# Two parts of the second layer's conditioning, computed in the first layer's routing and at the layer boundary

## Chip, cores and metric

The kernel runs on one core of one Trainium2 chip. The metric is the device time of one execution in microseconds (us). Times are compared by the median of repeated runs; a profile is one further execution, recorded by the hardware profiler.

## What is computed

Two layers of a hybrid backbone over 256 latent tokens and 256 context tokens of 1024 features, all in f32. Cut to what matters here:

```python
for i in range(DEPTH):                                   # DEPTH = 2
    mod = (silu(c) @ ada_w[i] + ada_b[i])[:, None, :]    # conditioning: 1024 x 6144 per layer
    mod_c = silu(c_ctx) @ ada_w[i] + ada_b[i]
    sh1, s1, g1, sh2, s2, g2 = split(mod, 6)             # and the same of mod_c
    px = modulate(rms(x, norm1[i]), sh1, s1) @ w_in[i]   # modulate(h, b, a) = h * (1 + a) + b
    pc = modulate(rms(ctx, norm1[i]), sh1c, s1c) @ w_in[i]
    yx, yc = mixers(px, pc, ...)                         # retention, windowed GQA, global GQA
    x = x + g1 * (yx @ w_out[i])
    hx = modulate(rms(x, norm2[i]), sh2, s2)
    ...                                                  # layer 0: the same for the context
    x = x + g2 * moe(hx, w_router, b_router, w_gate_up[i], w_down[i])   # top 2 of 16 experts
```

The conditioning of a layer is needed in three stages: `sh1, s1` before the input projection, `g1, sh2` after the output projection, `s2, g2` for the router and the end of the experts.

## The kernel before

**Stages.** Each layer runs norm1, the input projection `px` in five column blocks (3, 0, 4, 1, 2), the three mixers, `out_proj` with the router's product at its end, `route`, and the experts (`moe`). Layer 1 needs no context output after the mixers. Large products are made of two rounded halves of each f32 operand and three matmuls (`mm3`, L200 to L202); the halves of a weight page are `hi` on ACT (L190) and `lo` on DVE (L192), for the first `w_in` pages of layer 1 on POOL.

**Weights.** All weights come as pages of 1 MB in one order, the list `stream` that `run` writes; SP issues the loads (L164) in that order, each as soon as a page of SBUF is free. `take` waits for a page, `drop` gives it back and lets `pump` issue the next load. SP is one queue: an instruction of SP that waits holds up all behind it, also the stores `hx` (L1015) of the normalized tokens, which the experts' gather (L1224, POOL) reads back. The list stops at the second expert's pages until the order of the experts is known.

**Conditioning.** `ada_w` of a layer is cut in three thirds of 8 pages: third (l, 0) holds `sh1, s1`, (l, 1) `g1, sh2`, (l, 2) `s2, g2`. A third is 16 small bias matmuls (L362), then 8 steps of four 32-column matmuls (L347; the trace has two records for each) into the tile `adap`, then `ada_done`: a copy `adam` out of PSUM (L401, DVE), four transposes `modT` (L394), and small work on DVE. For third 0 this is `A` and `B` (L407, L409); for third 2 it is a memset and two DMAs of `n2` on POOL, one operation (L418), four DMAs `modd` on POOL and the router matrix `wm` (L429). The table `FILL` says how many steps run in each part of the mixers: thirds (0,1) and (0,2) in layer 0's `px` and attention, (1,0) in its retention (two steps per head), (1,1) in its global attention, and (1,2) in layer 1's `px`.

**Names in the order of work.** `rs` and `ro` (L796, L815) are the score and output products of a retention head, `am` (L800) the masked scores that `ro` reads, `s` the attention scores. `lg` and `lgT` (L956, L1005) are the router's logits and their transposes, `pos` (L1094) the positions of tokens in their experts, `over` (L1133) a number that all engines load before a branch, `fl` (L1294) the first expert's transposes. `fin` (L1566) and `ftmp` (L1577, L1578) end layer 0's experts; `junk` (L475) are the squares of norm1, `xT` (L493) its transposes; `hm` and `hT` (L512 to L519) the modulated input of layer 1, in four pairs of feature blocks; `tab` (L575 to L589) tables of the attention, on POOL.

Of the kernel before, what the change touches and what calls it, by code (L numbers as in the profile page):

```python
# [24 lines left out]
NPAGES = 20  # L25
RING = 6

FILL = [dict(px=1, att=8, ret=2, glb=8), dict(px=1, att=0, ret=0, glb=0)]

# [29 lines left out]
class Kernel:  # L61
    def __init__(self, nc, tc, es, I, out):
        self.nc, self.tc, self.I, self.out = nc, tc, I, out
        pool = lambda name, bufs=1, **k: es.enter_context(tc.tile_pool(name=name, bufs=bufs, **k))
        self.cp = pool("const")
        self.pgs = Pages(pool("pages"), NPAGES)
        self.hip = pool("hi")
        self.sm = pool("small", 2)
        self.ps = pool("psum", space=bass.MemoryType.PSUM)
        self.dr = pool("dram", space=bass.MemoryType.DRAM)  # L70
        self.flight = {}
        self.order = {}
        self.at = None
        self.spare = self.extra = 0
        self.hold = None
        self.owed = []
        self.ev = 0


# [66 lines left out]

    def pump(self):
        g = self.pgs
        while self.stream and (g.ring or self.extra < self.spare and g.open):
            c = self.stream[0]  # L150
            if c[0] in ("gu", "dn") and c[2] and c[1] not in self.order:
                break
            self.stream.popleft()
            src, k = self.chunk_src(c)
            if not g.ring:
                self.extra += 1
            i, t = g.tile((g.ring or g.open).popleft(), "w")
            dst = t if k is None else t.rearrange("p (k n) -> p k n", k=8 if k == "ada" else k)
            if k == "ada":
                dst = dst.rearrange("p k (s n) -> p k s n", s=2)  # L160
                for q in range(2):
                    self.nc.sync.dma_start(dst[:, :, q], src[:, :, q])
            else:
                d = self.nc.sync.dma_start(dst, src)  # L164
                if self.hold:
                    self.tc.add_manual_dep(d.ins, self.hold.ins.name, mybir.DependencyInfo(
                        mybir.DependencyClass.Sync, mybir.DependencyReason.DATA), reason="behind the gather")
                    self.hold = None
            self.flight[c] = i, t
# [168 lines left out]
                g.memset(self.rowsof[:, l, e:e + 1], 1.0)  # L338


    def ada_step(self, l, th, k):
        nc = self.nc
        i, t = self.take("ada", l, th, k)
        if k == 0:
            self.ada_bias(l, th)
        for j in range(4):
            nc.tensor.matmul(self.adap[j * 32:(j + 1) * 32], self.both(k), t[:, j * 512:(j + 1) * 512],  # L347
                             start=False, stop=k == 7)
        self.drop(i)
        if k == 7:  # L350
            self.ada_done(l, th)

    def both(self, k):

        return self.cT[:, 2 * k:2 * k + 32]

    def ada_bias(self, l, th):
        self.adap = self.bank("C", "adap")
        for j in range(4):
            for q in range(4):  # L360
                n = (l * 12 + th * 4 + j) * 4 + q
                self.nc.tensor.matmul(self.adap[j * 32:(j + 1) * 32, q * 128:(q + 1) * 128],  # L362
                                      self.ident[0:96, n:n + 1].to_broadcast([96, 32]), self.bias[0:96], start=q == 0, stop=False)
# [30 lines left out]
            self.nc.tensor.transpose(p[:, q * 128:(q + 1) * 128], m[:, q * 128:(q + 1) * 128], self.ident)  # L394
        return p.rearrange("p (q j r) -> p q j r", q=4, j=4)

    def ada_done(self, l, th):
        nc = self.nc
        v = nc.vector
        m = self.sm.tile([128, 512], F32, tag="sig", name="adam", bufs=2)  # L400
        v.tensor_copy(m, self.adap)  # L401
        if th == 0:
            A, B = self.AB[l] = self.cp.tile([128, 8, 2], F32, name=f"A{l}"), self.cp.tile([128, 8, 2], F32, name=f"B{l}")
            pv = self.columns(m)
            for j in range(2):
                k = slice(j * 4, j * 4 + 4)
                v.tensor_copy(B[:, k], pv[:, :, j, 0:2])  # L407
                gain = self.n1col[:, l * 8 + j * 4:l * 8 + j * 4 + 4, None].to_broadcast([128, 4, 2])
                v.scalar_tensor_tensor(A[:, k], pv[:, :, 2 + j, 0:2], 1.0, gain, op0=OP.add, op1=OP.mult)  # L409
            return  # L410
        nr = 2 - l
        if th == 2:

            n2 = self.sm.tile([128, 512], F32, tag="sig", name="n2", bufs=2)[0:64]
            nc.gpsimd.memset(n2, 0.0)
            for j in range(2):
                nc.gpsimd.dma_start(n2[j * 32:j * 32 + 2], self.I["norm2"][l, j * 512:(j + 1) * 512].partition_broadcast(2))
            v.scalar_tensor_tensor(m[0:64], m[0:64], 1.0, n2, op0=OP.add, op1=OP.mult)  # L418
        for j in range(4):
            c0 = th * 2048 + j * 512  # L420
            nc.gpsimd.dma_start(self.modd[l, 0:nr, c0:c0 + 512], m[j * 32:j * 32 + nr])

        pv = self.columns(m)
        if th == 2:
            self.wm[l] = self.sm.tile([128, 8, 2, 32], F32, tag="wm", name="wm", bufs=1)
            v.memset(self.wm[l], 0.0)
            for k in range(8):
                for r in range(nr):
                    v.tensor_scalar(self.wm[l][:, k, r, 0:16], self.wr[:, k], pv[:, k % 4, k // 4, r:r + 1], None, op0=OP.mult)  # L429
        else:  # L430
            sc = self.tiny("shc", [128, 8, 2], bufs=1)
            v.tensor_copy(sc.rearrange("p (j q) r -> p j q r", j=2), pv[:, :, 2:4, 0:2].rearrange("p q j r -> p j q r"))

            pc = self.bank("B", "c0")
            for k in range(8):
                nc.tensor.matmul(pc[0:16, 0:nr], self.wr[:, k], sc[:, k, 0:nr], start=k == 0, stop=k == 7)
            d = self.tiny("c0d", [16, 2, 16], bufs=1)
            for r in range(nr):
                v.tensor_scalar(d[:, r], self.ident[0:16, 0:16], pc[0:16, r:r + 1], None, op0=OP.mult)
            nc.tensor.matmul(pc[:, 32:32 + nr * 16], self.ones32, d[:, 0:nr].rearrange("p r e -> p (r e)"), start=True, stop=True)  # L440
            self.c0[l] = self.tiny("c0", [128, 2, 16], bufs=2)
            v.tensor_copy(self.c0[l][:, 0:nr], pc[:, 32:32 + nr * 16].rearrange("p (r e) -> p r e", r=nr))
# [5 lines left out]
    def ada_fill(self, n):  # L448
        for _ in range(n):
            self.ada_step(*self.fill.popleft())  # L450


    def clear(self, after):

# [9 lines left out]
    def norm1(self, l):  # L464
# [6 lines left out]
        for i in range(parts * 4):  # L471
            n, t = (i // 4, i % 4) if l else (i % 2, i // 2)
            o = (t % 2) * 1024 + n * w
            with self.tc.issue_after(self.kept.ins) if l and n > 0 else nullcontext():
                nc.scalar.activation(tmp[:, o:o + w], self.x[t][:, n * w:(n + 1) * w], AF.Square, accum_out=ss[:, t, n:n + 1])  # L475
        s1 = self.tiny("ss1s", [128, 4])
        nc.vector.tensor_reduce(s1, ss[:, :, 0:parts], axis=AX.X, op=OP.add)
        r = self.rsqrt(s1, D, [128, 4], "n1")
# [429 lines left out]
    def out_proj(self, l):  # L908
# [94 lines left out]
        p = self.bank("B", "lgT")  # L1003
        for t in range(nt):
            nc.tensor.transpose(p[:, t * 128:(t + 1) * 128], lgs[:, t * 128:(t + 1) * 128], self.ident)  # L1005
        lg = self.tiny("lgt", [128, 4, 16], bufs=1)
        pv = p.rearrange("p (t j e) -> p t e j", t=4, j=4)
        v.tensor_reduce(lg[:, :nt], pv[:, :nt, 0:16, :], axis=AX.X, op=OP.add)
# [18 lines left out]
    def route(self, l, lg, row):  # L1027
# [114 lines left out]
        if l:  # L1142
            self.early = [self.bank("CB"[b], "pl") for b in range(2)]
            for b in range(2):
                self.place(self.early[b], self.oh[0], b)
        self.overflow(l)
        perm = sq()
        v.tensor_tensor(perm, rank[:, None, :].to_broadcast(b16), self.rho[:, l, :, None].to_broadcast(b16), op=OP.is_equal)
        v.tensor_tensor(c3, perm, self.eid[:, None, :].to_broadcast(b16), op=OP.mult)
# [478 lines left out]
def run(K):  # L1628
# [3 lines left out]
    K.HX = [K.dr.tile([512 if l < DEPTH - 1 else 256, 1024], F32, name=f"hx{l}") for l in range(DEPTH)]  # L1632
    K.Y = [K.dr.tile([512 if l < DEPTH - 1 else 256, 1024], F32, name=f"y{l}") for l in range(DEPTH)]
    ada = [("ada", l, th, k) for l in range(DEPTH) for th in range(3) for k in range(8)]
    st, f = [], deque(ada[8:])
    K.fill = deque(x[1:] for x in f)

    def some(n):
# [2 lines left out]

    for l in range(DEPTH):
        fill = FILL[l]
        for n in (3, 0, 4, 1, 2):
            for h in range(2):
                if l == 0 and n == 3:
# [8 lines left out]
        for n in range(2):  # L1655
            for h in range(2):
                st.append(("w_out", l, n, h))
        gu, dn = ([[(kind, l, e, j) for j in range(n)] for e in range(NE)] for kind, n in (("gu", 8), ("dn", 4)))
        st += gu[0] + dn[0] + gu[1]
        for e in range(2, NE):  # L1660
# [10 lines left out]
    for l in range(DEPTH):  # L1671
        if l:
            K.norm1(l)
            K.qk_tables(l)
        K.mixers(l)
        lg, row = K.out_proj(l)
        K.route(l, lg, row)
        K.moe(l)
# [33 lines left out]
```

## Time and profile before

| | |
|---|---|
| timed runs | 1613.36, 1615.36, 1615.17 us |
| median | 1615.17 us |
| the profiled execution | 1607.81 us, its span 1606.0 us |
| layer 0: mixers, output projection, route | 0 to 266, 266 to 331, 331 to 354 us |
| layer 0: experts | 354 to about 885 us |
| layer 1: norm1, `px` and mixers | 885 to about 1050 us |
| layer 1: output projection and route; experts | to 1100; to 1606 us |
| TensorE busy, DVE busy, ACT busy, POOL busy | 90 %, 50 %, 35 %, 9 % |

The shares are means over stages with different limits. In the experts the DMA engines are near full for long stretches; in the mixers TensorE is. The granted clock of TensorE is full nearly everywhere and half in the routes and around the boundary between the layers.

### The profile page before, as it was taken

How to read it: one execution, taken by the hardware profiler on the slowest of the kernel's cores; microseconds unless marked ns; L12 is line 12 of the kernel's file. 1: busy time of each engine (PE TensorE's matmuls, PEld its weight loads, DVE VectorE, ACT ScalarE, POOL GpSimd, SP SyncE). 2: the span in 40 equal slices, each digit the busy share in tenths (PEclk: the TensorE clock that was granted, in tenths of full speed). 3: DMA queues.
4: the chain of work that ended last, by engine and by line, in shares of the span. 5: the costliest groups of instructions: out<-in, count | busy, mean ns of one | idle time of the engine just before them, and what ended most of it. 6: DMA issues, size and time to landing. Idle time of an engine off the chain costs nothing. (4 is left out here: it accounts for less than half of the span.)

```text
span 1606.0 us, 20671 instructions
## 1 busy us (share of the span) xinstructions
PE 1451.1 (90%) x7434; PEld 872.1 (54%) x7434; DVE 799.9 (50%) x1604; ACT 562.4 (35%) x864; POOL 139.5 (9%) x195
## 2 busy tenths in 40 slices
PE   5999999929999999989877799977999999999996
PEld 4767765716755745646424567656545545543332
DVE  5676576386754745637203787967405214220003
ACT  3352504225643734626202455434304213220000
POOL 2000000311010010000000200020000000000010
PEclk9999999969999999999999899987999999999999
DMA  9764679528999999999899442745899999999997
GB/s 269 282 224 155 236 263 347 194 99 317 414 411 404 414 413 406 404 413 378 346 399 371 162 156 95 260 171 210 340 416 417 379 383 419 402 394 417 416 367 279
DMA packets 115541, 515.57 MB, mean 321 GB/s; under 512 B 13889, under 2 KB 40161, under 8 KB 61794
## 3 DMA queue, kind: packets, MB, share of 16 engines
q1 hardware_dynamic: 102176, 488.67, 77.3%
q0 software_dynamic: 7888, 17.42, 3.9%
q10 hardware_dynamic: 5362, 8.03, 1.5%
q8 instruction: 62, 1.02, 0.3%
q14 instruction: 53, 0.43, 0.1%
HBM read 502.71 MB, written 16.96 MB: 324 GB/s over the span
## 5 line engine op out<-in xcount | busy, mean ns | idle before, releaser
L192 DVE TENSOR_TENSOR lo<-w,hi 128x1024 fp32r<-128x1024 f32 x294 | 359.1, 1231 | 100.3 <-ACT hi L190 27.2
L190 ACT ACTIVATE hi<-w 128x1024 fp32r<-128x1024 f32 x296 | 309.7, 1059 | 142.5 <-PE gu L202 47.3
L1313 PE MATMUL gs<-w,ex 128*64 128x512 f32 x1408 | 320.2, 601 | 17.8 <-DMA w<-in_w_gate_up_dram 17.5
L1313 PEld LDWEIGHTS gs<-w,ex 128*64 128x64 f32 x1408 | 95.5, 137 | 206.4 <-issue 162.7
L1329 PE MATMUL ds<-w,ex 128*64 128x512 f32 x640 | 149.6, 601 | 8.5 <-DMA w<-in_w_down_dram 8.5
L1319 DVE TENSOR_TENSOR ex<-ex,gs 128x512 f32<-128x512 f32 x22 | 15.1, 688 | 261.6 <-PE gs L1313 261.6
L201 PE MATMUL gu<-lo,ex 128*128 128x512 f32 (+1 forms) x320 | 129.1, 403 | 1.2 <-DVE lo L192 1.0
L202 PE MATMUL gu<-hi,ex 128*128 128x512 f32 (+1 forms) x320 | 127.9, 400 | 0.0
L200 PE MATMUL gu<-hi,ex 128*128 128x512 f32 (+1 forms) x320 | 112.9, 407 | 11.3 <-ACT hi L190 9.7
L201 PE MATMUL px<-lo,hT 128*128 128x512 f32 (+1 forms) x304 | 114.8, 378 | 0.4 <-DVE lo L192 0.4
L200 PE MATMUL px<-hi,hT 128*128 128x512 f32 (+1 forms) x304 | 114.4, 382 | 0.3 <-ACT hT L518 0.3
L202 PE MATMUL px<-hi,hT 128*128 128x512 f32 (+1 forms) x304 | 114.2, 376 | 0.0
L1318 ACT ACTIVATE ex<-gs 128x512 f32<-128x512 f32 x22 | 13.1, 597 | 272.2 <-PE gs L1313 272.2
L1379 POOL DMA_INDIRECT y<-ex,ridx x28 | 44.0, 1572 | 623.7 <-ACT ex L1335 366.3
L1329 PEld LDWEIGHTS ds<-w,ex 128*64 128x64 f32 x640 | 41.1, 136 | 81.6 <-issue 59.6
L200 PEld LDWEIGHTS gu<-hi,ex 128*128 128x128 f32 (+1 forms) x320 | 58.4, 185 | 30.4 <-ACT hi L190 14.0
L201 PEld LDWEIGHTS gu<-lo,ex 128*128 128x128 f32 (+1 forms) x320 | 59.3, 185 | 21.1 <-DVE lo L192 4.5
L200 PEld LDWEIGHTS px<-hi,hT 128*128 128x128 f32 x304 | 57.0, 188 | 20.5 <-issue 5.0
L202 PEld LDWEIGHTS gu<-hi,ex 128*128 128x128 f32 (+1 forms) x320 | 59.1, 185 | 15.4
L201 PE MATMUL dn<-lo,ex 128*128 128x512 f32 (+1 forms) x160 | 66.1, 413 | 1.4 <-DVE lo L192 1.2
L202 PE MATMUL dn<-hi,ex 128*128 128x512 f32 (+1 forms) x160 | 64.5, 403 | 0.0
L201 PEld LDWEIGHTS px<-lo,hT 128*128 128x128 f32 x304 | 57.3, 188 | 12.5 <-issue 2.0
(350 smaller groups left out, 1897.3 us busy)
## 6 DMA issues: line engine op xcount, KB each, us to landing
w<-in_w_gate_up_dram SPq DMA_DIRECT2D x256, 1024.0 KB, 12.6
w<-in_w_down_dram SPq DMA_DIRECT2D x128, 1024.0 KB, 14.0
w<-in_ada_w_dram SPq DMA_DIRECT2D x40, 1024.0 KB, 6.6
w<-in_w_in_dram SPq DMA_DIRECT2D x20, 1024.0 KB, 7.4
w<-in_ada_w_dram SPq DMA_DIRECT2D x16, 512.0 KB, 8.3
w<-in_w_out_dram SPq DMA_DIRECT2D x8, 1024.0 KB, 6.6
y<-zero POOLq DMA_DIRECT2D x3, 1024.0 KB, 10.7
g<-modd ACTq DMA_DIRECT2D x6, 512.0 KB, 7.6
```

Of the source, the lines that this page charges most:

```text
L190: nc.scalar.activation(hi, w, AF.Copy)
L192: (nc.gpsimd if after else nc.vector).tensor_tensor(lo, w, hi.bitcast(F32), op=OP.subtract)
L200: mm(o, a[0], b[0], start=first, stop=False)
L201: mm(o, a[0], b[1], start=False, stop=False)
L202: mm(o, a[1], b[0], start=False, stop=last)
L1313: nc.tensor.matmul(ps[n // 2][(n % 2) * 64:(n % 2) * 64 + 64], x[:, self.part(k)], t[:, n * 512:(n + 1) * 512], start=k == 0, stop=k == 7)
L1318: nc.scalar.activation(h, ps[0], AF.Silu)
L1319: nc.vector.tensor_tensor(h, h, ps[1], op=OP.mult)
L1329: nc.tensor.matmul(p[n * 64:n * 64 + 64], self.sx[2][:, self.part(ff)], t[:, f * 1024 + n * 512:f * 1024 + n * 512 + 512], start=ff == 0, ...
L1379: self.nc.gpsimd.indirect_dma_start(out=dst, out_offset=bass.IndirectOffsetOnAxis(ap=idx, axis=0), in_=y, in_offset=None, bounds_check=n - ...
```

## The change

Third (1,0) leaves layer 0's retention and third (1,2) leaves layer 1's `px`. The eight pages of (1,0) are loaded behind `w_out` of layer 0 and ahead of the first expert's pages; its bias and 32 matmuls stand behind the transposes `lgT` of layer 0's routing, in PSUM bank A. The eight pages of (1,2) stand at the head of layer 1's list, ahead of `w_in`; its bias and matmuls stand in norm1 of layer 1, behind the squares. For both, ACT makes the copy `adam`, and the rest of `ada_done` waits in a list that `ada_late` empties: before the branch on `over` in layer 0, and behind norm1 in layer 1. While `quiet` is set (from step 5 of (1,0) on, until behind the branch) `pump` issues no load. The numbers of matmuls and of loaded bytes stay.

```diff
-FILL = [dict(px=1, att=8, ret=2, glb=8), dict(px=1, att=0, ret=0, glb=0)]
+FILL = [dict(px=1, att=8, ret=0, glb=8), dict(px=0, att=0, ret=0, glb=0)]
...
-        while self.stream and (g.ring or self.extra < self.spare and g.open):
+        while self.stream and not self.quiet and (g.ring or self.extra < self.spare and g.open):
...
-    def ada_step(self, l, th, k):
+    def ada_step(self, l, th, k, bank="C", late=False):
...
         if k == 7:
-            self.ada_done(l, th)
+            if late:
+                m = self.hip.tile([128, 1024], F32, tag="hl", name="adam", bufs=5)[:, 0:512]
+                nc.scalar.activation(m, self.adap, AF.Copy)
+                self.late.append(partial(self.ada_done, l, th, m))
+            else:
+                self.ada_done(l, th)
...
+    def ada_ahead(self, third, bank):
+
+        for k in range(8):
+            self.ada_step(*third, k, bank, True)
+            self.quiet = bank == "A" and k >= 5
+
+    def ada_late(self):
+        while self.late:
+            self.late.pop(0)()
...
+        if l:
+            self.ada_ahead((1, 2), "C")
         s1 = self.tiny("ss1s", [128, 4])
...
             nc.tensor.transpose(p[:, t * 128:(t + 1) * 128], lgs[:, t * 128:(t + 1) * 128], self.ident)
+        if l == 0:
+            self.ada_ahead((1, 0), "A")
...
+        self.ada_late()
         self.overflow(l)
+        self.quiet = False
+        self.pump()
...
-    st, f = [], deque(ada[8:])
+    third = lambda l, th: [("ada", l, th, k) for k in range(8)]
+    st, f = [], deque(third(0, 1) + third(0, 2) + third(1, 1))
...
+        if l:
+            st += third(1, 2)
         for n in (3, 0, 4, 1, 2):
...
+        if l == 0:
+            st += third(1, 0)
         gu, dn = ([[(kind, l, e, j) for j in range(n)] for e in range(NE)] for kind, n in (("gu", 8), ("dn", 4)))
...
             K.norm1(l)
+            K.ada_late()
             K.qk_tables(l)
```

**Where the order of TensorE moves in layer 0.** Lines of the changed kernel stand some 20 higher than those of before (L956 becomes L976, L1005 becomes L1025, L347 becomes L349). TensorE in layer 0's retention, before: `adap_1965` is third (1,0), between the products of the heads.

```order
L796 MATMUL rs_1919<-rt_729 128x512
L362 MATMUL adap_1965<-bias_235,ident_79 32x128 x16
L347 MATMUL adap_1965<-w_1662,cT_107 32x512 x4
L347 MATMUL adap_1965<-w_1696,cT_107 32x512
L394 MATMUL modT_1881<-ident_79,adam_1870 128x128 x4
L815 MATMUL ro_1923<-rv_1561,am_1904 128x128 x12
L347 MATMUL adap_1965<-w_1696,cT_107 32x512 x3
L796 MATMUL rs_1994<-rt_729 128x256
```

The same place after:

```order
L816 MATMUL rs_1919<-rt_729 128x512
L816 MATMUL rs_1965<-rt_729 128x256
L816 MATMUL rs_1968<-rt_729 128x256
L816 MATMUL rs_1971<-rt_729 128x512
L816 MATMUL rs_1975<-rt_729 128x512
L401 MATMUL modT_1881<-ident_79,adam_1870 128x128 x4
L835 MATMUL ro_1923<-rv_1561,am_1904 128x128 x12
L835 MATMUL ro_1979<-rv_1561,am_1905 128x128 x12
```

The third is gone from here, and the scores of the second head follow at once on those of the first. SP around layer 0's route, after (before, all pages of the first expert, `w_gate_up` x8 and `w_down` x4, stood ahead of the stores `hx`):

```order
L166 DMA w_2736<-in_ada_w_dram 128x2048
L166 DMA w_2762<-in_w_gate_up_dram 128x2048
L166 DMA w_2764<-in_w_gate_up_dram 128x2048
L166 DMA w_2832<-in_w_gate_up_dram 128x2048
L166 DMA w_2885<-in_w_gate_up_dram 128x2048
L166 DMA w_2976<-in_w_gate_up_dram 128x2048
L166 DMA w_2964<-in_w_gate_up_dram 128x2048
L166 DMA w_2970<-in_w_gate_up_dram 128x2048
L166 DMA w_2982<-in_w_gate_up_dram 128x2048
L166 DMA w_2988<-in_w_down_dram 128x2048
L166 DMA w_2994<-in_w_down_dram 128x2048
L1037 DMA hx0_73<-xr_2544 128x1024 x2
```

The last six loads ahead of `hx` take pages that steps 0 to 5 of the third give back in the route itself; two of the first expert's twelve pages come behind the store. ACT at the boundary, after (before, the halves `hi` of this first `w_in` page stood among the squares of norm1, ahead of the modulation):

```order
L538 ACTIVATE hT_7576<-hm_7623 128x512
L355 ACTIVATE adam_7550<-adap_7485 128x512
L538 ACTIVATE hT_7576<-hm_7633 128x512
L532 ACTIVATE hm_7643<-xT_7638,B1_3110,A1_3109 128x256
L192 ACTIVATE hi_7722<-w_7518 128x1024
L538 ACTIVATE hT_7577<-hm_7643 128x512
L532 ACTIVATE hm_7653<-xT_7648,B1_3110,A1_3109 128x256
L192 ACTIVATE hi_7754<-w_7518 128x1024
```

They stand now in the fourth of the four modulation pairs. POOL there, after: the table work of attention comes first, then

```order
L429 DMA modd_72<-adam_7550 16x1x32 x2
L194 TENSOR_TENSOR lo_7723<-w_7518,hi_7722 128x1024
L423 MEMSET n2_7658 64x512
L425 DMA n2_7658<-in_norm2_dram 2x512 x2
L194 TENSOR_TENSOR lo_7755<-w_7518,hi_7754 128x1024
L429 DMA modd_72<-adam_7550 16x1x32 x2
```

where before the two `lo` stood ahead of the table work, and the `n2` and `modd` work far behind it.

## Rows read from the trace of the kernel before

**Rows 1.** The page: 40 slices of 40.15 us; one group with its mean in ns.

```profile
PE   5999999929999999989877799977999999999996
...
DMA  9764679528999999999899442745899999999997
...
L190 ACT ACTIVATE hi<-w 128x1024 fp32r<-128x1024 f32 x296 | 309.7, 1059 | 142.5 <-PE gu L202 47.3
```

**Rows 2.** Busy time in stretches: length, each engine, granted clock, DMA share, GB/s.

```profile
core 0: us, PE busy (x) PEld busy (x) DVE busy (x) ACT busy (x) POOL busy (x), PEclk, DMA share, GB/s
202.80:239.57 36.77, 36.77 (x237) 22.22 (x237) 26.32 (x125) 1.31 (x3) 1.03 (x2) 1.00 0.72 260
...
1015.00:1045.00 30.00, 26.96 (x177) 21.27 (x175) 27.73 (x128) 11.31 (x26) 1.84 (x4) 1.00 0.63 231
```

**Rows 3.** TensorE in time, layer 0's retention: start, duration, operation, records.

```profile
202.80 2.13 PE L362 MATMUL adap<-bias,ident 96*32 96x128 f32 x29
...
214.40 1.04 PE L347 MATMUL adap<-w,cT 128*32 128x512 f32 x2
215.37 2.27 PE L815 MATMUL ro<-rv,am 128*128 128x128 f32 x18
217.58 1.92 PE L347 MATMUL adap<-w,cT 128*32 128x512 f32 x14
219.43 1.99 PE L796 MATMUL rs<-rt 64*128 64x256 f32 x6
```

**Rows 4.** All engines in time, layer 0's route; in brackets idle time and what ended it.

```profile
331.02 0.95 PE L1005 MATMUL lgT<-ident,lgs 128*128 128x128 f32 x4 [0.79 <-DVE lgs L959]
...
335.03 4.01 SPq L1015 DMA_DIRECT2D hx<-xr  x4
...
346.14 1.12 POOL L1224 DMA_INDIRECT ex<-hx,ridx  x1 [17.62 <-DVE rcap L1124]
...
353.72 1.08 PE L1294 MATMUL fl<-ident,ex 128*128 128x128 f32 x4 [8.68 <-PEq L1399]
```

**Rows 5.** Stretches of the route and the first dense products behind it, columns as in rows 2.

```profile
345.00:356.00 11.00, 1.13 (x6) 0.71 (x4) 5.55 (x21) 2.51 (x3) 1.70 (x2) 0.50 0.13 37
356.00:368.60 12.60, 8.55 (x27) 6.01 (x28) 10.07 (x17) 4.83 (x6) 2.00 (x1) 0.50 0.40 151
368.60:374.00 5.40, 5.40 (x25) 4.32 (x23) 4.55 (x5) 3.55 (x5) 0.00 (x0) 0.98 1.02 423
```

**Rows 6.** All engines in time, the boundary between the layers.

```profile
877.29 1.28 DVE L1578 TENSOR_TENSOR ftmp<-ftmp,g 128x512 f32<-128x512 f32 x2
...
879.66 2.38 POOL L192 TENSOR_TENSOR lo<-w,hi 128x1024 fp32r<-128x1024 f32 x1 [39.63 <-ACT hi L190]
...
881.28 4.08 DVE L1578 TENSOR_TENSOR ftmp<-ftmp,g 128x512 f32<-128x512 f32 x2
...
895.13 2.58 PE L493 MATMUL xT<-ident,junk 128*128 128x128 f32 x11 [10.15 <-DVE junk L99]
...
901.31 0.50 PE L200 MATMUL px<-hi,hT 128*128 128x512 f32 x1
...
908.94 1.02 ACT L512 ACTIVATE hm<-xT,B,A 128x256 f32<-128x256 f32 x2 [1.36 <-DVE hm L514]
```

**Rows 7.** Stretches of the boundary, columns as in rows 2.

```profile
885.00:895.10 10.10, 0.00 (x0) 0.00 (x1) 8.58 (x24) 4.31 (x17) 4.45 (x10) 0.63 0.97 359
...
901.30:920.00 18.70, 18.29 (x103) 14.94 (x103) 12.04 (x20) 11.13 (x23) 0.00 (x0) 1.00 0.35 113
```

**Rows 8.** TensorE and DVE in time, the rest of third (1,2) in layer 1.

```profile
942.33 2.78 PE L347 MATMUL adap<-w,cT 128*32 128x512 f32 x24
...
1006.08 1.06 PE L347 MATMUL adap<-w,cT 128*32 128x512 f32 x8
...
1013.88 0.69 DVE L401 COPY adam<-adap 128x512 f32<-128x512 f32 x1
...
1018.92 1.23 DVE L429 TENSOR_SCALAR wm<-wr,modT 128x16 f32<-128x16 f32 x8 [0.81 <-PE modT L394]
```

More of the change, by code (lines that the diff above doesn't have):

```diff
@@ L76, in __init__ @@
         self.owed = []
+        self.late = []
+        self.quiet = False
         self.ev = 0
@@ L344, in ada_step @@
         if k == 0:
-            self.ada_bias(l, th)
+            self.ada_bias(l, th, bank)
         for j in range(4):
@@ L350, in ada_step, with ada_bias @@
         if k == 7:
-            self.ada_done(l, th)
+            if late:
[4 more added lines that the diff above has]
+                self.ada_done(l, th)
     def both(self, k):
         return self.cT[:, 2 * k:2 * k + 32]
-    def ada_bias(self, l, th):
-        self.adap = self.bank("C", "adap")
+    def ada_bias(self, l, th, bank):
+        self.adap = self.bank(bank, "adap")
         for j in range(4):
@@ L395, in columns, with ada_done @@
         return p.rearrange("p (q j r) -> p q j r", q=4, j=4)
-    def ada_done(self, l, th):
+    def ada_done(self, l, th, m=None):
         nc = self.nc
         v = nc.vector
-        m = self.sm.tile([128, 512], F32, tag="sig", name="adam", bufs=2)
-        v.tensor_copy(m, self.adap)
+        if m is None:
+            m = self.sm.tile([128, 512], F32, tag="sig", name="adam", bufs=2)
+            v.tensor_copy(m, self.adap)
         if th == 0:
@@ L1145, in route @@
                 self.place(self.early[b], self.oh[0], b)
+        self.ada_late()
         self.overflow(l)
+        self.quiet = False
+        self.pump()
         perm = sq()
```

## The prediction, made before the changed kernel ran

> **What bounds the kernel now.** I read the page's slices first [rows 1]. TensorE is at nine tenths in most of them, and the DMA engines are full in the two long stretches of the experts. So a shift of the start of the experts is carried to their end one for one, and a microsecond is won or lost only in what stands ahead of them: mixers, route, boundary. Next the stretches. In layer 0's retention, where third (1,0) lies, TensorE is busy 36.77 of 36.77 us and DVE 26.32 [rows 2]: TensorE is the bound, DVE the next. In layer 1's mixers, once all conditioning is done, it is the other way round: DVE 27.73 of 30 us, TensorE 26.96 [rows 2]. Then the route [rows 4, 5]: TensorE waits for DVE nearly throughout and the clock is half (0.50). The room into which (1,0) is put is real there. Last the boundary [rows 6, 7]: TensorE does nothing from 885 to 895.1, and the DMA engines are full (0.97) in that very gap.
>
> Everything below is summed against the profiled run, 1607.81 us (span 1606.0 and 1.8 around it). The median of the runs, 1615.17, lies 7.4 us higher; I add the sum to the median.
>
> **Part A, third (1,0) leaves the retention.** Its eleven groups on TensorE, each counted from its start to the start of what follows, as 214.40 to 215.37 (0.97 us for only two records) and 217.58 to 219.43 (1.85 for fourteen) [rows 3], make 13.7 us with the bias [rows 3] and the transposes. So 36.8 - 13.7 = 23.1 us of TensorE are left. DVE keeps 26.32 less the copy `adam` (0.69, the same operation as in [rows 8]), 25.6 us, and so becomes the bound. Without conditioning in between, DVE reached 27.73 / 30 = 0.92 in layer 1 [rows 2]; 25.6 / 0.92 = 27.7 us. Gain 36.8 - 27.7 = **9.1 us**. The ends: 13.7, if DVE's work slides past the end of the stretch; 5, if the order within a head decides. The two-record groups stand just where `ro` would wait for the masked scores, so that three times 0.97 us and about half of the other 11 us of filler only turn into idle time. I take 9.1, since `rs` of two heads now stand together and the layer 1 row has the same chain.
>
> **Part B, third (1,0) enters the route.** The matmuls themselves are covered: TensorE waited there for DVE. Three things are not. First, 12 bias matmuls and one conditioning matmul stand ahead of `lgT`, about 0.8 + 0.4 = 1.2 us by their pitch in the retention, and all of DVE's route hangs on `lgT` [rows 4]. Second, four small operations of `A` and `B` stand ahead of the cast `over`, on which the branch waits: 4 x 0.16, and up to 1 us for the transposes they need. Third, the stores `hx` were issued at 335.03 [rows 4]; now SP must first issue six loads, each behind a step of the third, and the last behind step 5. At 423 GB/s a page takes 2.5 us [rows 5], so six take 15; from the first freed page at about 334 that is 349, and `hx` lands some 3 us later, against a gather that was issued at 346.14 and is read by `fl` at 353.72 [rows 4]. The gather then goes out near 352 and `fl` starts near 357. The two ways are parallel; the later one counts: **+3.5 us**. Ends: +1, if `hx` shares the engines with the loads instead of following them and only the branch is late; +8, if the steps run at half clock and step 5 ends only at 344. The two `w_down` pages that now come behind the store go through engines that were almost idle (0.13) up to 356 [rows 5]; at no cost, or 2.5 us if they push the second expert's first page.
>
> **Part C, third (1,2) at the boundary.** Steps 0 to 4 stand ahead of `xT` and lie in TensorE's empty 10.1 us [rows 7], five times 1.0 us; their pages are the first five loads there, which were issued by 882 in the order of before. The eight loads are moved ahead of `w_in`, and with that its halves move too. Before, both `lo` of the first half page ran on POOL during the experts' end, and an `ftmp` pair on DVE took 4.08 us beside them, where the pair just ahead took 1.28 [rows 6]; that slow pair goes, a gain of 2.5. But now `hi` stands on ACT behind the first operation of the fourth modulation pair: 908.94 + 0.5 [rows 6] + 1.06 for `hi` [rows 1] = 910.5, less 2.5 = 908.0, where `px` started at 901.31 [rows 6]. The first column block then took 18.7 us, to 920.0 [rows 7]; eight conditioning records in it, 2.0 us, are gone, but the first product with `lo` waits for POOL's 2.38 us [rows 6], of which the four products with `hi` cover 0.9: 908.0 + 18.7 - 2.0 + 1.6 = 926.3, **+6.3 us**. The second `lo` stands behind the memset and two `n2` DMAs on POOL; it is wanted only half a block later, some 8 us, and that covers it. Behind the `modd` DMAs, which wait for ACT's `adam`, stands only that. Ends: 0, if ACT and the modulation run ahead of what I took over from before; +9, if the slow pair merely moves.
>
> The granted clock fell in the empty stretch (0.63 over 885 to 895 [rows 7]) and was full again in the block of `px`. In the route it stayed half until 368.6, though the products began at 356.4 [rows 5]. [...]
>
> **Part D, the rest of layer 1.** From 920 on, 48 records of third (1,2) leave `px`, in groups as in [rows 8]: by starts 2.7 + 1.0 + 1.0 + 1.0 + 1.0 us and 0.4 of waiting for a page, 7.1, with `modT` 0.5. On DVE, `adam` 0.69, the scaling 0.67, `wm` 1.23 and 0.81 of idle before it [rows 8] leave the stretch that DVE bounds. The last three groups stand in solid runs of matmuls and count in full, 3.0; of the earlier 4.1 about 2.2, since DVE is nearly as busy there; of DVE's 3.4 I take 1.3. **-6.5 us**, between -3 and -10.5.
>
> Sum: -9.1 + 3.5 + 6.3 - 6.5 = -5.8, that is 1602.0 for the profiled run and **1609.4** for the median.
>
> **Rivals.** *The retention gives little back.* If the chain within a head decides (the low end of A, 5 us), the sum is -1.7 and the time 1613.5. For it: DVE is at 0.72 there and its waits are for `rs` and `ro`. Against it: the filler often runs while DVE is busy with the head before.
>
> *px starts late and slowly; slower than before.* The place is the first block of layer 1. TensorE is empty from the end of `xT` until `hi` has come from ACT. If the clock falls in that gap and comes back only after 12.2 us, as behind the route (356.4 to 368.6, [rows 5]), 12.2 us do the work of 6.1: C becomes 12.4. If the fifth page is late as well, so that `xT` waits for step 4 (2.5 us), or the slow `ftmp` pair stays (2.5), it is 15 to 17.4. Against A, B and D (-12.1) it decides from 12.1 on, that is, when the second block starts later than 932. Time: about +4, 1619. For it: the half clock in the rows on both sides of such a gap. Against it: five steps now fill part of the earlier gap, and behind 895 the clock came back at once.
>
> *Both thirds vanish.* A at 13, B at 1.5, C at 2, D at -8: -17.5, 1597.7. For it: all engines have room at both new places. Against it: [rows 2] leave DVE no such room.
>
> **How the numbers follow.** The forecast, between -3.3 and -10, has 0.42; the first rival 0.25, the second 0.20, the third 0.13. A measurement tells about 0.2 %, 3.2 us, from no change. Faster by more is the forecast with the third rival, 0.55; within it the first, 0.25; slower the second, 0.20. The range reaches over most of the rivals: 1599 to 1620.
>
> **What would show it.** In the changed profile: the retention ends about 9 us earlier and DVE's share in it is over 0.9 (A); `fl` starts some 3.5 us later, counted from `lgT`'s place, with `hx` landing at the end of the six loads (B); the first `px` matmul waits for `hi` on ACT, and the second block starts 6 us later counted from the end of the experts (C); `px` of layer 1 from there to the output projection is 6.5 us shorter (D). The forecast is wrong if TensorE's idle time in the retention grows as much as the filler shrinks, if `fl` waits long for the gather, or if the granted clock is half in the first block of `px`.

## The result, and the profile after the change

The changed kernel is slower. Its median is 1621.65 us against 1614.26 for the kernel before in the same series: half a per cent more. The recorded ratio is 1.0058, with an interval of 1.0033 to 1.0082 (the quotient of the two medians alone is 1.0046). The prediction, 1609.4 with a range of 1599 to 1620, had the wrong sign, and the time lies outside the range. The profiled execution took 1616.96 us (span 1615.2) where that of before took 1607.81 (1606.0).

Where did the 9.2 us of span come from? The table follows the same event through both traces, each by the start of its instruction. Its first row stands ahead of anything that the change touches on TensorE: the single executions differ by up to 5 us there (200.0 to 205.1 over the kernels of this document), so the rows below are best read as differences to it.

| event | before, us | after, us | difference |
|---|---|---|---|
| first `rs` of layer 0's retention | 200.0 | 201.5 | +1.5 |
| first output projection matmul, layer 0 | 267.1 | 255.5 | -11.6 |
| cast `over` ahead of the branch | 348.0 | 335.3 | -12.7 |
| `fl`, first expert | 353.7 | 349.3 | -4.4 |
| first page load behind the branch | 362.4 | 354.2 | -8.2 |
| first `w_down` load behind it | 406.3 | 404.7 | -1.6 |
| last `fin` of layer 0's experts | 881.9 | 878.1 | -3.8 |
| first `px` of layer 1 | 901.3 | 903.1 | +1.8 |
| first `qkT` (end of the first column blocks) | 929.5 | 934.0 | +4.5 |
| first `rs` of layer 1's retention | 1013.7 | 1014.2 | +0.5 |
| last output projection matmul | 1072.0 | 1076.1 | +4.1 |
| `over` of layer 1 | 1091.3 | 1094.6 | +3.3 |
| end | 1606.0 | 1615.2 | +9.2 |

So some 13 us are won in the retention (from its first `rs` on), 10 of them are lost again by the first `w_down` load, the boundary takes 8, and the rest of layer 1's mixers gives next to nothing back. The page shows it in its slices, now of 40.4 us (PE, granted clock, DMA; tenths):

```profile
PE   5999999939999999999878889878999999999996
PEclk9999999959999999999999899998999899999999
DMA  9764657587999999999999623445999999989997
```

Against [rows 1] the ninth slice, the route, has 3 for 2, since conditioning now runs in it. From the 19th slice on nine tenths and eight tenths change places here and there, and no stage stands out: the loss is a few microseconds in several places, so it is read from the stretches below.

**The retention** (columns as in rows 2):

```profile
201.52:237.00 35.48, 35.33 (x240) 23.19 (x236) 30.61 (x146) 4.98 (x12) 2.07 (x4) 1.00 0.44 152
237.00:255.47 18.47, 15.54 (x100) 8.76 (x98) 16.72 (x47) 10.97 (x28) 1.96 (x4) 1.00 1.04 404
```

TensorE stays full in the first stretch, at the work of the next mixer, and DVE becomes the bound only in the second (16.72 of 18.47, 0.91). In the first stretch no idle time took the filler's place; in the second TensorE is idle for 2.9 us.

**The route** (stores and gather, then TensorE and SP behind them; in brackets idle time and what ended it), and below it the times from issue to landing of the stores `hx` of after, then those of before; each trace has the landing of two of the four stores:

```profile
326.07 1.91 SPq L1037 DMA_DIRECT2D hx<-xr  x4
344.74 1.13 POOL L1249 DMA_INDIRECT ex<-hx,ridx  x1 [18.45 <-SPq L1424]
349.31 1.09 PE L1319 MATMUL fl<-ident,ex 128*128 128x128 f32 x4 [15.17 <-DMA ex<-hx,ridx]
354.21 2.21 SPq L166 DMA_DIRECT2D w<-in_w_gate_up_dram  x4
363.33 0.66 PE L1310 MATMUL tu<-ident,ex 128*128 128x128 f32 x2 [5.02 <-DMA ex<-hx,ridx]
...
DMA to landing us min/median/max: 12.6/14.4/16.3
...
DMA to landing us min/median/max: 2.7/2.8/2.8
```

The stores leave 9 us earlier than in [rows 4] but land 12.6 to 16.3 us later: the page loads issued ahead of them fill the DMA engines (share 1.05 from 338 to 342). The gather, which was issued ahead of the branch in [rows 4], now stands behind it (POOL's branch at 336.71 here, at 348.75 before). And one thing is new altogether: two of the four `tu` (transposes of the second expert's rows, before at 382.17) now stand at 363.33, behind only eight products of the first expert, and wait 5 us for the second gather.

**The boundary** (ACT, POOL, DVE, TensorE in time), then its first 10 us of `px`:

```profile
899.96 0.59 ACT L355 ACTIVATE adam<-adap 128x512 f32<-128x512 f32 x1
902.00 1.04 ACT L192 ACTIVATE hi<-w 128x1024 fp32r<-128x1024 f32 x1
903.10 1.65 PE L202 MATMUL px<-hi,hT 128*128 128x512 f32 x4 [5.38 <-ACT hi L192]
903.13 2.36 POOL L194 TENSOR_TENSOR lo<-w,hi 128x1024 fp32r<-128x1024 f32 x1 [1.17 <-ACT hi L192]
903.59 2.45 DVE L539 TENSOR_TENSOR hT<-hm,hT 128x512 fp32r<-128x512 f32 x1 [0.90 <-ACT hT L538]
905.54 0.80 PE L203 MATMUL px<-lo,hT 128*128 128x512 f32 x1 [0.80 <-POOL lo L194]
...
903.00:913.00 10.00, 9.11 (x31) 7.39 (x32) 4.03 (x4) 3.86 (x7) 7.38 (x7) 0.62 0.55 185
```

`px` waits 5.38 us for `hi` on ACT, and then the granted clock is 0.62 over its first 10 us, at the half level (0.50) from 900.4 to 910.6, where before it was 1.00 in the first block [rows 7].

**Layer 1's mixers.** The waits of TensorE from 934 to 1076 (first rows: total, times, longest), then the stretch of [rows 2]:

```profile
PE s L686 <- ACT P L697: 4.0, 4, 2.4
PE rs L816 <- DVE am L820: 2.3, 1, 2.3
...
1015.00:1045.00 30.00, 25.04 (x146) 18.05 (x145) 25.76 (x113) 10.75 (x20) 0.00 (x0) 1.00 0.40 143
```

Before, the largest wait of TensorE there was 1.7 us, for a normalization of DVE.

### The profile page after: what moved, and what is told of

Same layout as the page of the kernel before. It is cut to its first block, busy times and chain, and to the rows that moved or that the text cites. A ratio compares the mean times of both kernels' runs of the same rounds, so it can differ in the third digit from the quotient of the medians.

```text
span 1615.2 us, 20668 instructions
## 1 busy us (share of the span) xinstructions
PE 1455.9 (90%) x7434; PEld 881.1 (55%) x7434; DVE 796.8 (49%) x1602; ACT 564.6 (35%) x866; POOL 139.3 (9%) x195
## 5 line engine op out<-in xcount | busy, mean ns | idle before, releaser
L1343 ACT ACTIVATE ex<-gs 128x512 f32<-128x512 f32 x22 | 13.1, 597 | 276.2 <-PE gs L1338 276.2
L202 PEld LDWEIGHTS gu<-hi,ex 128*128 128x128 f32 (+1 forms) x320 | 58.2, 184 | 29.6 <-ACT hi L192 14.2
L1282 PEld LDWEIGHTS pl<-oh,xr 128*128 128x128 f32 x416 | 52.6, 205 | 23.5 <-ACT ex L95 10.6
```

What stands on the lines that cost most here:

```text
L202: mm(o, a[0], b[0], start=first, stop=False)
L1282: nc.tensor.matmul(p[:, self.part(k)], self.xr[t][:, k * 128:(k + 1) * 128], oh[:, t, 0:64], start=t == k == 0, stop=t == nt - 1 and k == 7)
L1343: nc.scalar.activation(h, ps[0], AF.Silu)
```

## Experiments

Two theories stood against each other at first. Mine after the two traces: each part loses by itself, the route by `tu` and the late rows, the boundary by `hi` behind `adam`. The rival: the parts are harmless alone and hurt only together, through the order of the pages.

### One part alone

Only (1,0) moved (`e1_only_route`):

```diff
-FILL = [dict(px=1, att=8, ret=0, glb=8), dict(px=0, att=0, ret=0, glb=0)]
+FILL = [dict(px=1, att=8, ret=0, glb=8), dict(px=1, att=0, ret=0, glb=0)]
-            self.ada_ahead((1, 2), "C")
-            st += third(1, 2)
```

with third (1,2) appended to the list of fillers.

> Only third (1,0) is moved, into the route; third (1,2) stays in px of layer 1 as before. Theory (what the retention gives, 12 us, is lost again in the route, since the stores hx stand behind six weight loads and two transposes tu of the second expert's rows wait for a gather): output projection starts 11 to 12 us earlier than before, fl only 4 us, the loads of the third expert under 2 us; total within 3 us of before, ratio 0.998 to 1.001. Rival 1 (the route alone makes the change slow): ratio 1.004 or more. Rival 2 (the boundary alone does, and the route's loss is small): 6 us faster or more, ratio under 0.9965.

Measured: 1610.86, ratio 0.9997 (0.9975 to 1.0019). The output projection starts 7.9 us earlier (259.2), but `w_down` behind the first expert's pages is issued at 407.97, 1.7 us later than before. In this execution the retention itself began 5.0 us later than in that of before (first `rs` at 205.1); counted from there it gives 12.9 us, and 3.3 of them are left at `w_down`, as in after (3.1). Most of the gain is lost within the route and the first expert, with no boundary part in it, and the total is that of my theory.

Only (1,2) moved (`e2_only_boundary`: `ret=2` back in `FILL`, no `ada_ahead((1, 0), ...)`, third (1,0) among the fillers).

> Only third (1,2) is moved, to the boundary; third (1,0) stays in the retention of layer 0 as before. Theory: px of layer 1 starts 5 us later counted from the end of the experts, runs its first 8 us at half clock, and what leaves px later turns into idle time in layer 1's retention; slower by 4 to 8 us, ratio 1.0025 to 1.005. Rival (what leaves px pays for the late start, as the prediction had it): within 2 us.

Measured: 1621.61, ratio 1.0072 (1.0048 to 1.0095), at the high end of what I expected and beyond. `fin` ends as before (882.0), and all of the loss comes behind it. The profile repeats that of after:

```profile
907.12 1.65 PE L202 MATMUL px<-hi,hT 128*128 128x512 f32 x4 [5.28 <-ACT hi L192]
907.00:917.00 10.00, 9.08 (x31) 7.36 (x32) 3.93 (x4) 3.78 (x7) 7.03 (x7) 0.61 0.74 252
1022.97 1.13 PE L816 MATMUL rs<-rt 64*128 64x256 f32 x4 [2.24 <-DVE am L820]
```

The parts add up (-0.03 % and +0.72 % against +0.58 %, inside the intervals): each is judged by itself from here on.

### The route: the stores, or the transposes?

`e3_hx_act` lets the stores of layer 0 go out from ACT's queue instead of SP's:

```diff
-            nc.sync.dma_start(self.HX[l][t * 128:(t + 1) * 128, :], xr[t])
+            (nc.sync if l else nc.scalar).dma_start(self.HX[l][t * 128:(t + 1) * 128, :], xr[t])
```

> The changed kernel, with the four stores hx of layer 0 issued on ACT's queue and not behind the loads on SP's; the transposes tu come back to their old place with it. Theory: hx lands in under 8 us, not 12.6 to 16.3, the gather goes out at about 338 and fl follows the branch at about 341; the experts start some 7 us earlier than in the changed kernel, ratio to before 0.999 to 1.002. Rival (the stores share the same 16 engines with the loads, so another queue does not help): the gather stays at 344 and only the wait of tu goes; ratio 1.003 to 1.006.

Measured: 1621.27, ratio 1.0073 (1.0050 to 1.0097). The stores still land late, and the gather waits as long (landing of two of the four stores, gather, `fl`); POOL's wait for all four ends at 342.9:

```profile
DMA to landing us min/median/max: 12.0/12.4/12.7
...
343.88 1.12 POOL L1249 DMA_INDIRECT ex<-hx,ridx  x1 [18.93 <-SPq L1424]
352.86 1.09 PE L1319 MATMUL fl<-ident,ex 128*128 128x128 f32 x4 [19.59 <-DMA ex<-hx,ridx]
```

So it is not SP's queue alone that holds the stores, which is the rival's account; that the page loads ahead of them do, whichever queue they are issued from, is seen in `e5_hx_first` and `e7_route_tu_hx` below, where they land after 4.5 to 4.8 us with the loads held back. In this kernel `tu` fell back to its old place by itself, and two more page loads went out ahead of the gather's data, so that its total isolates nothing.

`e4_tu_back` leaves the changed kernel as it is and only ties the four `tu` behind the fifth step of the first expert; `e6_route_tu` does the same to `e1_only_route`:

```diff
-        mm(o, a[1], b[0], start=False, stop=last)
+        self.last_mm = mm(o, a[1], b[0], start=False, stop=last)
-                    self.pick_up(l, e + 1, k - 5)
+                    with self.tc.issue_after(self.last_mm.ins) if not last and not e else nullcontext():
+                        self.pick_up(l, e + 1, k - 5)
```

> The changed kernel, with the transposes tu of the second expert's rows tied behind the fifth step of the first expert's product, where they stood before; hx stays on SP's queue. Theory: the 5.0 us wait of TensorE for the second gather goes, and the loads of the third expert come 3 to 5 us earlier; ratio to before 1.002 to 1.005. Rival (the next thing, the halves of the late weight pages, ends at the same time): no difference to the changed kernel, 1.0058.

> Only third (1,0) is moved into the route, and tu stays at its old place; third (1,2) stays in px of layer 1. Theory (the boundary is the loss, and the route keeps 7 us once tu does not wait): third expert's loads 6 to 7 us earlier than before and so to the end, ratio 0.9945 to 0.997. Rival (the experts, paced by the DMA engines, give the start back): within 2 us of before.

Measured: `e4_tu_back` 1613.07, ratio 1.0025 (1.0000 to 1.0050); `e6_route_tu` 1599.11, ratio **0.9936** (0.9911 to 0.9960), faster than both kernels and than my range for it. Of `e6_route_tu`, TensorE and SP:

```profile
348.14 1.09 PE L1317 MATMUL fl<-ident,ex 128*128 128x128 f32 x4 [14.44 <-DMA ex<-hx,ridx]
372.84 0.60 PE L1308 MATMUL tu<-ident,ex 128*128 128x128 f32 x4
396.97 9.22 SPq L166 DMA_DIRECT2D w<-in_w_down_dram  x4
```

`fl` waits 14.44 us as in after, yet `w_down` is issued at 396.97 instead of 406.27 in the trace of before: 9.3 us earlier, and 10 us at the end. Against `e1_only_route` the tie is worth 0.6 %, and the intervals stay apart. Besides the four `tu`, twelve products of the first expert, one `lo` and four `idx` change places with their neighbours; the order of the rest stays. For `e4_tu_back` the intervals overlap (1.0000 to 1.0050 against 1.0033 to 1.0082), but its trace shows the same: from the first load behind the branch to `w_down` it takes 43.9 us, in after 50.5, before 43.9.

### Why the wait at `fl` costs so little

`e5_hx_first` (from `e4_tu_back`) and `e7_route_tu_hx` (from `e6_route_tu`) hold the page loads back until the stores have been issued; then four go, and the rest behind the branch ("the run before it" in the second expectation is `e6_route_tu`):

```diff
         for k in range(8):
+            self.quiet = bank == "A"
             self.ada_step(*third, k, bank, True)
-            self.quiet = bank == "A" and k >= 5
...
             row(3)
+            if l == 0:
+                self.quiet, self.left = False, 4
+                self.pump()
```

> The changed kernel with tu at its old place, and with the loads that take the third's pages held back until the stores hx are issued (then four, the other four behind the branch). Theory (the loads ahead of hx keep the gather and the branch waiting): hx lands within 6 us, the gather goes out ahead of the branch again, fl starts at about 345 where the kernel with tu alone had 350.3; 3 to 5 us faster than that kernel, ratio to before 0.999 to 1.001. Rival (the branch and the late pages end at the same time anyway): no difference to it, 1.0025.

> As the run before it, and with the loads held back behind the stores hx. Theory: another 3 to 5 us at fl, ratio 0.992 to 0.996. Rival (the pages that come later then hold up the first expert or the loads behind them): the same as without, 0.9945 to 0.997, or slower than it.

Measured: 1614.43, ratio 1.0035 (1.0013 to 1.0057), and 1598.05, ratio 0.9934 (0.9910 to 0.9957); both like the kernel that each was made from. The stores now land 4.5 to 4.8 us after their issue, in both. Of `e7_route_tu_hx`, in time:

```profile
343.74 1.09 PE L1323 MATMUL fl<-ident,ex 128*128 128x128 f32 x4 [9.20 <-DMA ex<-hx,ridx]
344.96 1.23 DVE L1188 TENSOR_TENSOR pm<-sq,rpr 128x1024 f32<-128x1024 f32 x1 [8.12 <-PE fl L1323]
349.49 0.68 DVE L1332 TENSOR_TENSOR ex<-fl,ex 128x512 fp32r<-128x512 f32 x1
353.51 44.36 SPq L167 DMA_DIRECT2D w<-in_w_gate_up_dram  x16
```

`fl` starts 4.4 us earlier than in `e6_route_tu`, but the first load behind it at 353.51 against 353.13. The rows of DVE tell why: between `fl` and the second half `ex` of the rows that the first expert needs, DVE has four operations of 1.2 us for the indices of the second expert (344.96 to 349.5). In `e6_route_tu` DVE starts them at 345.58, and two are done and the third is running when `fl` starts at 348.14. So there the wait is filled with work that TensorE would wait for otherwise. In `e7_route_tu_hx` DVE begins them only behind `fl` (8.12 us idle until it), 0.6 us earlier for a `fl` that is 4.4 earlier; why DVE waits for `fl` there, no run shows. The same order explains the table: from `fl` to the first load it takes 8.7 us before and 4.9 after.

### The boundary: the order of the pages, or the place?

`e8_w_in_first` (from `e2_only_boundary`) loads the first `w_in` page ahead of the third, so that `hi` and `lo` could be made early:

```diff
-            st += third(1, 2)
...
+                if l and n == 3 and h:
+                    st += third(1, 2)
```

> Only third (1,2) is moved to the boundary, but the first w_in page is loaded ahead of the third and not behind it. Theory (px waits at the boundary because its first halves come from ACT and POOL behind the modulation): px starts within 2 us of before counted from the end of the experts, the clock is full in its first block, and at least 5 of the 11.7 us that this part alone cost come back; ratio 1.001 to 1.004. Rival (the loss is that what leaves px only turns into idle time in layer 1's retention, whose order moved): 1.005 or more.

Measured: 1623.53, ratio 1.0100 (1.0063 to 1.0136); my theory fell in that form, and the time is that of the rival. The page was there, but on ACT `hi` still stood behind `adam`:

```profile
907.46 0.59 ACT L355 ACTIVATE adam<-adap 128x512 f32<-128x512 f32 x1
908.98 2.00 ACT L192 ACTIVATE hi<-w 128x1024 fp32r<-128x1024 f32 x2
910.09 1.65 PE L202 MATMUL px<-hi,hT 128*128 128x512 f32 x4 [6.65 <-ACT hi L192]
```

In the code `adam` takes its tile from the five buffers of the halves. `e10_w_in_first_adam_own` gives it one of another group:

```diff
-                m = self.hip.tile([128, 1024], F32, tag="hl", name="adam", bufs=5)[:, 0:512]
+                m = self.sm.tile([128, 512], F32, tag="P", name="adam", bufs=3)
```

> Only third (1,2) is moved, the first w_in page is loaded ahead of it, and the copy adam has a tile of a group of its own and not one of the group that the halves hi and lo take in turn; with that hi stands among the squares again. Theory (px waited because hi may not take its tile before adam has had its own, so that hi came behind the third's last step and the modulation): px starts within 3 us of where it starts before, counted from the end of the experts, at full clock, and 8 us or more of the last kernel's loss go; ratio 0.999 to 1.003. What is left against before is then the order of layer 1's retention, about 5 us, less the 3 us that px saves. Rival (px waits for the modulation or for POOL): px stays 5 us late, ratio 1.005 or more.

Measured: 1622.59, ratio 1.0062 (1.0037 to 1.0087). `hi` is back among norm1's squares and `px` starts at 901.4, as before and at full clock, but the ratio is that of the rival and the loss stays:

```profile
877.33 1.05 ACT L192 ACTIVATE hi<-w 128x1024 fp32r<-128x1024 f32 x1
919.77 0.83 PE L401 MATMUL modT<-ident,adam 128*128 128x128 f32 x4 [3.00 <-DVE adam L426]
915.00:920.00 5.00, 2.00 (x11) 1.54 (x10) 0.79 (x1) 1.01 (x1) 2.31 (x8) 1.00 1.06 375
```

The conditioning now stands inside the first blocks of `px`, its pages come late (DMA 1.06), and its end holds up TensorE there. So the tile group explains why `hi` was late, and not why the part loses.

`e11_all_mended` is the changed kernel with all three mends (`tu`, `w_in` first, `adam` in its own group).

> The changed kernel with all three mends: tu at its old place, the first w_in page ahead of third (1,2), adam out of the halves' group. Theory (the parts add): the 10 us of the kernel that moves only third (1,0) with tu in place, and what the boundary part comes to alone, 0 to +4 us: ratio 0.993 to 0.997. Rival (the boundary loses by where it is, whatever the order): 1.000 or more.

Measured: 1612.75, ratio 0.9994 (0.9974 to 1.0015). Against `e6_route_tu`, which differs by the boundary part alone, about 0.6 % is lost: the parts do not add as the theory said, and the time lies between it and the rival. The two traces are alike up to `px`; then, by differences between the starts of the same events:

| stretch | `e6_route_tu`, us | `e11_all_mended`, us |
|---|---|---|
| last `fin` to first `px` | 19.3 | 19.4 |
| first `px` to first `qkT` | 28.2 | 36.2 |
| first `qkT` to first `rs` | 84.4 | 81.0 |
| first `rs` to last `po` | 58.3 | 64.8 |

## Why the prediction was wrong, step by step

**A, the retention: the gain was sized too small, and DVE was not the bound.** 9.1 us were forecast, because DVE's work in the stretch would bound it, with an end of 13.7 "if DVE's work slides past the end of the stretch". From the first `rs` to the first output projection it takes 54.0 us instead of 67.1: 13.1 less, nearly all of the 13.7 that left (12.2 to 13.1 in the eight kernels with this part). The end of the range happened: TensorE ran the next mixer ahead of DVE and stayed full, with DVE at 0.86 in the first stretch and over 0.9 only in the second. The first rival, that the retention gives little, is refuted by the same rows.

**B, the route: the first step that failed.** I summed it to +3.5 and its upper end to +8. From the last router product (-12.3) to `fl` (-4.4) the loss is 7.9. On the clock of before, the stores were issued at 338.4, far ahead of my 349, but then took 12.6 to 16.3 us to land where I had 3; the gather fell behind the branch, and `fl` starts at 361.6 (349.3 + 12.3) where I had 357. The 1.2 us ahead of `lgT` came as 1.0. But `fl` turned out not to be the bound: 3.8 us come back right behind it, since DVE makes the next expert's indices during the wait. What decided was a step that the prediction doesn't have: two `tu`, not touched by the diff, stand early in TensorE's order and wait 5.02 us for the second gather, and the clock is at half until 367.9 where it is full from 358.6 on in `e6_route_tu`. From the first load (-8.2) to `w_down` (-1.6) that is 6.6 us, and together B came to +10.7. `e4_tu_back` and `e6_route_tu` put the transposes back, with few other moves, and those 6.6 us go; the totals gain 0.3 % and 0.6 %. With `tu` in its place, A and B together are worth 10 us, more than the 5.6 that I gave them.

**C, the boundary: the second rival's mechanism, at a smaller price.** `hi` behind `adam`, the first step of C, is as foretold, and `px` starts 25.0 us after `fin` instead of 19.4, +5.6. I had 908.0 - 901.3 = 6.7 for it. To that comes the slow first block: +2.7 more by `qkT`, together +8.3 against +6.3 and an end of +9 (in that sum, 1.6 should be 2.38 - 0.9 = 1.5). The forecast had taken the full clock of the first block from [rows 7]; the rival's condition, an empty stretch ahead of `px`, was met (idle from 897.7 to 903.1), and the clock was at half from 900.4 to 910.6, 7.5 us of it in `px`. The rival had 12.2 us of it and C at 12.4 or more; the second block starts 8.3 us later, not 12.1, so by its own sign it did not decide alone. I had set against it that the clock came back at once behind 895; in the trace of before it is at half until 897.8. So at this place the granted clock is half in part of such a gap and behind it in both traces, for 2.6 us before and 7.5 in after; no run isolates what lowers it or what brings it back. The slow `ftmp` pair of [rows 6] did go: no `ftmp` of after took more than 0.69 us, where one before took 2.85, and `lo` now starts at 903.13, behind the last of them (start at 881.7).

**D, the rest of layer 1: the second step that failed, -6.5 forecast, -0.4 measured.** The conditioning left `px`, and the stretch from `qkT` to `rs` is 4.0 us shorter. But from `rs` to the last `po` it is 3.6 us longer. Over both, from `qkT` to `po`, TensorE's busy time falls from 136.1 to 131.7 us, and the stretch only from 142.5 to 142.1: the filler turned into idle time. The rows of the first 22 us behind the first `rs`, with columns as in rows 2, and the last step of the masks `dm` (count, ns, first and last start), before and after:

```profile
1013.70:1036.00 22.30, 19.80 (x131) 16.49 (x128) 20.91 (x101) 8.49 (x18) 1.97 (x4) 1.00 0.59 217
L764 DVE TENSOR_TENSOR dm<-dm,mtmp x4: 551/558/559, 999.3 to 1012.0; 128x384 f32<-128x384 f32 x4
...
1014.20:1036.00 21.80, 19.13 (x109) 14.53 (x108) 17.14 (x77) 7.30 (x11) 0.00 (x0) 1.00 0.30 105
L784 DVE TENSOR_TENSOR dm<-dm,mtmp x4: 549/555/559, 1002.9 to 1016.5; 128x384 f32<-128x384 f32 x4
```

Before, DVE was the limit (20.91 of 22.30). Its masks `dm` were ready in time: the last starts at 1012.0, `rs` at 1013.7. After, TensorE is early and DVE is not: the last mask starts at 1016.5, 82.5 us behind the first `qkT` as it did before, while `rs` starts at 1014.2. The first masked scores come 2.9 us behind the first `rs` instead of 0.7, TensorE waits for them, and then both engines idle in turn, each waiting for the other. The filler's 6.7 us, taken from ahead of `rs`, were TensorE's alone; the masks that `rs` runs into did not come any sooner. I had written that [rows 2] "leave DVE no such room", as an argument against the third rival; in D I took only a part off for it (2.2 of the earlier 4.1 us) and counted the last three groups in full, 3.0.

After is the mildest case. In all eight kernels with the boundary part the last mask starts 2.3 us behind `rs`, where in the four without it starts 1.7 ahead of it; and in the other seven the granted clock falls to half right behind that wait, for 3.4 us in two of them and 6.8 in five. From `rs` to the last `po` these take 63.5 and 64.7 to 65.2 us, after 61.9, the four others 58.2 to 58.3. So of the 6.5 us that `e11_all_mended` loses there, about 3 go with the clock, an estimate from its half level between 1010.5 and 1017.3. `e10_w_in_first_adam_own` is one of the five:

```profile
1020.00:1030.00 10.00, 10.00 (x43) 7.98 (x44) 4.62 (x20) 1.38 (x3) 0.00 (x0) 0.70 0.29 105
```

**The experts of layer 1.** From `over` to the end the profiled run of after is 5.9 us longer, though the change doesn't touch this. Short stretches with the granted clock at half add up to 13.7 us before and 27.3 after; half of the difference, 6.8 us, would be lost by that, an estimate from the granted clock. One such stretch, before and after:

```profile
1400.00:1450.00 50.00, 47.13 (x247) 24.88 (x248) 12.73 (x17) 11.77 (x14) 2.98 (x2) 1.00 1.01 397
...
1400.00:1450.00 50.00, 46.27 (x212) 25.31 (x210) 12.72 (x16) 12.36 (x15) 2.98 (x2) 0.90 0.92 364
```

Over the twelve profiles this part grows with that sum, from 513.2 us at 10.2 to between 519.4 and 522.3 at 27.3. The sum does not go with either part of the change: `e8_w_in_first`, with the boundary part, has 13.7, `e1_only_route`, without it, 27.3. What sets it stays open; the medians differ by 7.4 us, the two profiled executions by 9.2.

By measured sizes the sum is +1.5 ahead of the retention, -13.1 in it, -0.7 from there to the last router product, +10.7 from there to `w_down`, -2.2 in layer 0's experts, +8.3 at the boundary and -0.4 behind it: +4.1, which is the table's row of the last `po`. B came out 7.2 us above its term, 6.6 of them the step that it doesn't have; D came out 6.1 above, C 2.0. Either of the first two alone takes my sum of -5.8 to about zero or above. The 4.0 us by which A was taken too small hide part of it.

## What to carry to other kernels

- When work moves to a new place, look in the changed order for instructions that the diff does not name and that have changed places on the busiest engine: here two transposes, under 1 us of work, cost 6.6 us, half of what the retention had won.
- Filler taken out of a stretch was worth here what the second busiest engine allowed: in layer 0's retention, with DVE at 0.72, 13.1 of 13.7 us came back; in layer 1, with DVE at 0.94 where the filler's room would have been, 0.4 of 7. And an idle wait was worth only what no other engine did during it: of the 7.9 us lost up to `fl`, 3.8 came back right behind it.
- Judge the parts of a change apart. One part here is worth 0.6 % with one tie added, the other costs 0.6 to 1.0 % in each of the orders tried.

## What the runs showed of the hardware

- The stores `hx`, 512 KB each, landed 12.6 to 16.3 us after their issue in after, behind page loads of 1024 KB, instead of 2.8 before; with the loads held back behind them they landed after 4.5 to 4.8 us (`e5_hx_first`, `e7_route_tu_hx`). Another engine's queue did not help: 12.0 to 12.7 us for the two stores that the trace of `e3_hx_act` has.
- The branch on TensorE's queue took 4.5 to 4.6 us in the four kernels with third (1,0) in its old place, and 6.0 to 6.7 in the eight with it in the route. Beside it the DMA share is 0.15 before (348.8 to 353.3), and 1.03 in after (336.7 to 343.4), where page loads are under way. No run isolates the loads as the cause. Before and after:

```profile
L1399 PEldq COMPARE_BRANCH  x1: 4523/4523/4523, 348.8 to 348.8; - x1
...
L1424 PEldq COMPARE_BRANCH  x1: 6723/6723/6723, 336.7 to 336.7; - x1
```

- DVE's `hT` at 903.59 took 2.45 us beside POOL's `lo` (903.13 to 905.49), where others of its form took 0.69; it ended at 906.04, some 0.6 us behind `lo`. No run isolates `lo` as the cause.
